# A two-layer decoder trunk: the last norm's output turned token by token on TensorE, fourteen products of ones ahead of the first chunk, and three steps of a key compression set one chunk further apart

## The chip, the cores and the metric

The kernel runs on one core of one Trainium2 chip. The metric is the device time of one execution in microseconds (us). A profiled execution also has a span, from its first to its last recorded event; times inside a profile count from the start of that span. TensorE is written PE (PEld for its weight loads), VectorE DVE, ScalarE ACT, GpSimd POOL and SyncE SP.

## The reference, cut to what matters

One sequence of 256 tokens with 2048 features runs through two layers: a mixer A (dilated attention), then a mixer B (compressed, selected and sliding-window attention over shared keys and values), each followed by an MLP and a gated per-layer embedding. The last thing computed is an RMSNorm over the 2048 features of each token.

```python
def reference(x, p, ...):
    h = x
    for i in range(DEPTH):
        hn = rmsnorm(h, attn_norm_g[i])
        ...                                   # mixer A (i = 0) or shared keys/values and mixer B (i = 1)
        hn = rmsnorm(h, mlp_norm_g[i])
        h = h + jnp.square(jax.nn.relu(hn @ mlp_w1[i])) @ mlp_w2[i]
        gate = jax.nn.sigmoid(rmsnorm(h, ple_norm_g[i]) @ ple_w_gate[i])
        h = h + (p[i] @ ple_w_proj[i]) * gate
    return rmsnorm(h, final_norm_g)
```

For mixer B, keys and values of 15 overlapping blocks of 32 tokens are compressed by a small MLP: a block's positions are flattened (`z`), multiplied by `w1`, passed through gelu and multiplied by `w2`; the keys are then rotated by position.

## The kernel before, in words

**Layout.** Activations lie features first: sixteen tiles `x[k]` of 128 features x 256 tokens in f32, held in eight pair tiles `xp[j]` of 512 columns. Weights come from HBM in chunks of 128 x 1024 f32 (512 KB), some 870 of them, through one loop (`Program.run`).

**Precision.** An f32 weight chunk `raw` becomes two parts: ACT casts the high part (`whi`, L196), DVE subtracts to get the low part (`wlo`, L202). Activations are split likewise (`xa`, L289 and L293). A product is high x (high and low) plus low x high (`mm_tile`, L318 and L319; `token_major`, L401 to L403).

**Order of the work.** `Program.run` walks over a list of steps written out by hand. At each chunk it issues loads up to `DMA_AHEAD` = 7 chunks ahead (with four raw buffers, so a load waits for the low part made from that buffer's earlier tenant), casts and subtracts up to `SPLIT_AHEAD` = 3 chunks ahead (fewer in the first chunks), advances the generators that finish earlier chunks by one `yield`, and then issues the chunk's products. A generator that yields `"tensor"` is resumed only after that chunk's products, so a `yield` more means one chunk more between a producer and TensorE's use of it. Every engine runs its own instructions in the order in which they were issued.

**The start.** `start0` (L565) issues the loads of the first two halves of `xp[0]`; `load` (L181) issues each raw chunk and, behind it, the next pair tile of `x`, all on SP's queue. `pieces` (L189) cuts chunk 0 into two halves, for its load, its cast and its subtraction; all others go whole. The first eight chunks are a value projection of layer A in `token_major` form: 12 products of 512 columns a chunk.

**The compression.** In `compress` (chunk by chunk, alternating with the chunks of a value projection through `both`), the key's eight chunks come first, then the value's. `gelu` (L864) finishes each: copy out of PSUM, a product with `pair` that adds the two halves (L870), gelu on 64 x 256, two transposes (L886), then `comp_k` (L899): the second product (L902), the rotation on DVE, a transpose (L916), and the split into the key tiles that the scores of mixer B read. The generators of the key's chain run while the value's chunks are being multiplied.

**The end.** The last quarter of the gate projection runs feature tile by feature tile (`single`); its last tile, `one_half=True`, accumulates all in 256 columns. `last_gate` (L492) then works out one long chain: the gate for tile 15 (L497 to L501), its square (L220), the sum over features by products with a vector of ones, which gives one value per token in two columns (`column`, L234), the root on ACT (L241), a reciprocal and one Newton step on DVE (L247 to L250, the factor `col`, one value per token on 128 partitions x 2 columns). Since the output is features first, the factor must lie along the columns: DVE builds a diagonal matrix from it (L253), and a product of ones with that diagonal (`spread`, L257) spreads it over all partitions. DVE multiplies the tiles by it in nine pieces (L511), and SP and ACT issue the nine writes to `out` in turn (L512). The host then transposes `out`.

Of the kernel before, what the change touches and what calls it, by code (L numbers as in the profile page):

```python
# [10 lines left out]
F32 = mybir.dt.float32  # L11
# [4 lines left out]
P = 128  # L16
D = 2048
T = 256
KT = D // P
# [10 lines left out]
CH = 1024  # L30
ROPE_SWAP = [(j + 16) % 32 for j in range(32)]

DMA_AHEAD = 7
SPLIT_AHEAD = 3
RAW_BUFS, HI_BUFS, LO_BUFS = 4, 6, 5
# [96 lines left out]
def kernel(ctx: ExitStack, tc: tile.TileContext, a: dict, out: bass.AP):  # L132
    nc = tc.nc
# [5 lines left out]
    stat = ctx.enter_context(tc.tile_pool(name="stat", bufs=2))  # L139
# [25 lines left out]
    xp = [xpool.tile([P, 2 * T], F32, name=f"x{j}") for j in range(KT // 2)]  # L165
    x = [xp[k // 2][:, k % 2 * T:(k % 2 + 1) * T] for k in range(KT)]
    ones = const.tile([P, P], F32, name="ones")
# [8 lines left out]
    def load_x(j, half=None):  # L176
        c = slice(0, 2 * T) if half is None else slice(half * T, (half + 1) * T)
        nc.sync.dma_start(xp[j][:, c], a["xT"][:, j * 2 * T:(j + 1) * 2 * T][:, c])
# [9 lines left out]

    def pieces(n):  # L189

        return [slice(0, CH // 2), slice(CH // 2, CH)] if n == 0 else [slice(0, CH)]

    def copy(n, t):
        hi = wpool.tile([P, CH], F32R, tag="hi", name="whi", bufs=HI_BUFS)
# [11 lines left out]
    class Norm:  # L206
# [19 lines left out]
                (eng or nc.vector).tensor_add(self.acc, self.acc, s)  # L226
            self.done += 1

        def column(self, parts):

            ps = banks2()[:, 0, :] if parity[0] else bank()
            for j in range(2):
                for i, p in enumerate(parts):
                    nc.tensor.matmul(ps[:, j:j + 1], p[:, j * P:(j + 1) * P], ones[:, :1],  # L234
                                     start=i == 0, stop=i == len(parts) - 1)
            return ps
# [3 lines left out]
            nc.vector.tensor_scalar(self.v, ps[:, :2], 1.0 / D, EPS, op0=ALU.mult, op1=ALU.add)  # L240
            nc.scalar.activation(self.z, self.v, AF.Sqrt)  # L241

        def invert(self):

            v, z = self.v, self.z
            y, r = (stat.tile([P, 2], F32, tag=n, name=n) for n in ("sy", "col"))
            nc.vector.reciprocal(y, z)  # L247
            nc.vector.tensor_mul(z, y, y)
            nc.vector.scalar_tensor_tensor(z, z, -0.5, v, op0=ALU.mult, op1=ALU.mult)
            nc.vector.scalar_tensor_tensor(r, z, 1.5, y, op0=ALU.add, op1=ALU.mult)  # L250
            self.diag = stat.tile([P, T], F32, tag="diag", name="diag", bufs=1)
            for j in range(2):
                nc.vector.tensor_scalar_mul(self.diag[:, j * P:(j + 1) * P], ident, r[:, j:j + 1])  # L253
            self.col = r

        def spread(self, ps):
            nc.tensor.matmul(ps[:, 128:128 + T], ones, self.diag, start=True, stop=True)  # L257
# [231 lines left out]
    def ple(layer, pg, xg, norm, nxt, norm2, last):  # L489
        pj = [None] * KT  # L490

        def last_gate(ps):  # L492

            k = KT - 1
            prog.until(lambda: norm2.done == k)
            t = tmp.tile([P, T], F32, tag="et", name="et", bufs=7)
            nc.vector.tensor_mul(t, ps[:, :T], norm.rb)  # L497
            nc.scalar.activation(t, t, AF.Sigmoid)
            nc.scalar.activation(warm, ones[:, :1], AF.Sqrt)
            nc.vector.tensor_mul(t, t, pj[k])  # L500
            nc.vector.tensor_add(x[k], x[k], t)  # L501
            s = norm2.square(k, nc.vector)
            col = norm2.column([norm2.acc, s])
            norm2.root(col)
            nc.scalar.activation(x[k], x[k], AF.Identity, scale=gains[:, G_FIN, k:k + 1])
            norm2.invert()
            r = norm2.spread(col)
            for i, (k0, n) in enumerate([(0, 1), (1, 1)] + [(2 * j, 2) for j in range(1, KT // 2)]):
                y = xp[k0 // 2][:, k0 % 2 * T:(k0 % 2 + n) * T]
                y3 = y.rearrange("p (n t) -> p n t", t=T)  # L510
                nc.vector.tensor_mul(y3, y3, r[:, None, :].to_broadcast([P, n, T]))  # L511
                (nc.sync, nc.scalar)[i % 2].dma_start(out[:, k0 * T:(k0 + n) * T], y)  # L512
            return
            yield

        def gate_done(k, ps):
            t = sum_halves(ps)
            for _ in range(k % 4 // 2):
                yield
            while norm.r is None:  # L520
                yield
            nc.vector.tensor_mul(t, t, norm.rb)
            yield
            nc.scalar.activation(t, t, AF.Sigmoid)
            yield
            nc.vector.tensor_mul(t, t, pj[k])
            nc.vector.tensor_add(x[k], x[k], t)
            yield
            if last or k < 12:
                s = norm2.square(k)  # L530
                if last:
                    nc.scalar.activation(x[k], x[k], AF.Identity, scale=gains[:, G_FIN, k:k + 1])
                yield
                norm2.add(s)
            else:
                yield from renorm(k, G_KV, nxt, norm2)

        for q in range(4):
            def proj_done(f, ps, q=q):
                s = tmp.tile([P, T], F32, tag="es", name="es", bufs=4)  # L540
                nc.scalar.copy(s, ps[:, :T])
                t = cur["h"].tile([P, T], F32, tag="pj", name="pj", bufs=8)
                nc.vector.tensor_add(t, ps[:, T:], s)
                pj[4 * q + f] = t
                return
                yield
            quad(lambda c, q=q: a["w_proj"][layer * 4 + q], 2, pg, proj_done)
            hooks = {4: [norm.factor]} if q == 0 else {}
            if q == 3 and not last:
                for c in range(6):  # L550
                    hooks[c] = [lambda k=k: split_x(k, G_KV, nxt) for k in (2 * c, 2 * c + 1)]
            if q == 3 and last:
                for f in range(4):
                    single(lambda c, f=f: a["w_gl"][2 * f + c], xg,
                           (lambda ps, k=12 + f: gate_done(k, ps)) if f < 3 else last_gate,
                           ring=lambda: banks2()[:, 0, :], one_half=f == 3)
            else:
                quad(lambda c, q=q: a["w_gate"][layer * 32 + q * 8 + c], KT, xg,
                     lambda f, ps, q=q: gate_done(4 * q + f, ps), hooks)
# [5 lines left out]
    def start0():  # L565
        load_x(0, 0)
        load_x(0, 1)
        open_pool("A")
        pa = cur["A"]
        cur["mA0"] = pa.tile([P, NGA * P], F32, name="mA0")  # L570
        cur["mA1"] = pa.tile([P, NGA * T], F32, name="mA1")
# [292 lines left out]
    def gelu(n, ps):  # L864
        s = tmp.tile([P, T], F32, tag="et", name="et", bufs=7)
        nc.scalar.copy(s, ps)
        yield
        yield "tensor"
        y = bank()[:64, :256]
        nc.tensor.matmul(y, pair, s, start=True, stop=True)  # L870
        yield
        t = tmp.tile([64, T], F32, tag="et", name="et", bufs=7)
        u = tmp.tile([64, T], F32, tag="et", name="et", bufs=7)
        nc.scalar.activation(t, y, AF.Square)
        yield
        nc.vector.tensor_scalar(t, t, 0.044715, 1.0, op0=ALU.mult, op1=ALU.add)
        nc.vector.tensor_mul(t, y, t)
        yield
        nc.scalar.activation(t, t, AF.Tanh, scale=math.sqrt(2.0 / math.pi))
        yield  # L880
        nc.vector.scalar_tensor_tensor(u, t, 1.0, y, op0=ALU.add, op1=ALU.mult)
        yield
        yield "tensor"
        ps = bank()
        for k in range(2):
            nc.tensor.transpose(ps[:, k * 64:(k + 1) * 64], u[:, k * P:(k + 1) * P], ident[:64, :64])  # L886
        yield
        if n == "k":
            uT = cur["B"].tile([P, P], F32, name="uT", tag="uT", bufs=1)
            nc.scalar.copy(uT, ps[:, :P])  # L890
        else:
            uT = cur["B"].tile([P, 8, 3, 16], F32, name="uT3")
            nc.scalar.copy(uT, ps[:, :P].rearrange("p (b n) -> p b n", n=16)[:, :, None, :]
                           .to_broadcast([P, 8, 3, 16]))
        yield
        yield "tensor"
        yield from (comp_k(uT) if n == "k" else comp_v(uT))

    def comp_k(uT):  # L899
# [10 lines left out]
        nc.vector.tensor_mul(w[:, 16:], kc[:, :16], zt["rcS"][:, 16:])  # L910
        nc.vector.tensor_mul(kc[:, :32], kc[:, :32], zt["rcC"])
        nc.vector.tensor_add(kc[:, :32], kc[:, :32], w)
        yield
        yield "tensor"
        ps = bank()
# [329 lines left out]
```

## Time and profile before

| What | us |
|---|---|
| Median of three timed runs | 2523.98 (2523.86 to 2524.05) |
| The profiled execution's own time | 2523.56 |
| Its span | 2521.8 |
| PE busy | 2502.3 |
| DVE busy | 1719.2 |
| ACT busy | 1339.7 |

Busy time is summed over the instructions of an engine. "Idle before" an instruction is shown with what released it, for instance `<-PE at L234`: the DVE instruction waited for a product at line 234. A row such as `L234 PE MATMUL at<-ones,acc 128*128 128x1 f32 x4` is four records of a product that writes tile `at`, reads moving operand `ones` and stationary operand `acc`; an f32 product is recorded as two. Products are pipelined, so the distance between their starts says more than their lengths. The rows of a windows view give for each stretch its length, the busy time and the count of each engine, then PEclk (the granted TensorE clock as a share of full speed), the DMA share and GB/s.

### The profile page before, as it was taken

Reading aid. Unit: us, or ns where it says so; the run is one execution under the profiler, and the core shown is the slowest. Engines: PE = TensorE matmul, PEld = TensorE weight load, DVE = VectorE, ACT = ScalarE, POOL = GpSimd, SP = SyncE. Lnnn points to the kernel's source line nnn. Section 1 sums busy time; section 2 is a strip of 40 time slices with the busy share of each in tenths; the row PEclk is TensorE's granted clock in tenths of the full one; section 3 lists DMA queues with packets and bytes.
Section 4 is the critical chain, followed back from the end, with each engine's and each line's share of the span. In section 5 each row is a group of like instructions: output and inputs, shape, how many; then the busy total and the mean of one; then the engine's idle time right before and its main releaser. Section 6 shows DMA issues by size and latency. Waiting matters only on the chain.

```text
span 2521.8 us, 37917 instructions
## 1 busy us (share of the span) xinstructions
PE 2502.3 (99%) x14399; PEld 2198.0 (87%) x14399; DVE 1719.2 (68%) x3005; ACT 1339.7 (53%) x2146; POOL 10.4 (0%) x24
## 2 busy tenths in 40 slices
PE   9999999999999999999999999999999999999997
PEld 7888888888888888888888889888888888888887
DVE  6766677866566665567787989776656556556777
ACT  6444444554354453455564788655435445445555
POOL 0000000000000000000000000000000000000000
PEclk9999999999999999999999999999999999999999
DMA  7555555566666666566566754456666666666663
GB/s 265 175 177 180 172 164 177 176 187 191 189 189 191 192 187 191 191 190 187 186 198 191 243 159 125 142 189 186 191 191 189 189 190 191 190 189 191 191 185 118
DMA packets 129831, 466.23 MB, mean 185 GB/s; under 512 B 14576, under 2 KB 15600, under 8 KB 129648
## 3 DMA queue, kind: packets, MB, share of 16 engines
q1 hardware_dynamic: 128400, 461.76, 58.7%
q8 instruction: 113, 1.85, 0.3%
q0 software_dynamic: 528, 1.07, 0.2%
q10 hardware_dynamic: 720, 0.98, 0.1%
q14 instruction: 70, 0.57, 0.1%
HBM read 461.65 MB, written 2.10 MB: 184 GB/s over the span
## 4 chain that ended last, share of the span: by engine, by line
PE 99%; DVE 1%; DMA 0%; issue 0%; ACT 0%; SPq 0%; DVEq 0%
PE mm L318 31%; PE at L318 26%; PE mm L319 16%; PE at L319 13%; PE mm L403 1%; PE mm L401 1%; PE mm L402 1%; PE at L401 1%; PE at L402 1%; PE at L403 1%; PE at L1092 0%; PE at L635 0%; PE mm L1116 0%; PE mm L855 0%; PE mm L856 0%; PE mm L688 0%
## 5 line engine op out<-in xcount | busy, mean ns | idle before, releaser
L202 DVE TENSOR_TENSOR wlo<-raw,whi 128x1024 fp32r<-128x1024 f32 (+1 forms) x874 | 1065.1, 1220 | 623.6 <-PE at L319 242.1
L196 ACT CAST whi<-raw 128x1024 fp32r<-128x1024 f32 (+1 forms) x874 | 920.3, 1054 | 914.6 <-PE at L318 407.7
L318 PE MATMUL mm<-xa,whi 128*128 128x512 f32 x2176 | 766.4, 396 | 0.0
L319 PE MATMUL mm<-xa,wlo 128*128 128x256 f32 x2176 | 608.8, 280 | 0.0
L318 PE MATMUL at<-xa,whi 128*128 128x512 f32 x1648 | 573.6, 392 | 0.0
L318 PEld LDWEIGHTS mm<-xa,whi 128*128 128x128 f32 x2176 | 407.9, 187 | 92.6 <-issue 0.4
L319 PE MATMUL at<-xa,wlo 128*128 128x256 f32 x1648 | 461.1, 280 | 0.0
L319 PEld LDWEIGHTS mm<-xa,wlo 128*128 128x128 f32 x2176 | 410.8, 189 | 0.4
L318 PEld LDWEIGHTS at<-xa,whi 128*128 128x128 f32 x1648 | 308.3, 187 | 68.0
L318 PE MATMUL mm<-h,whi 128*128 128x512 f32 x1024 | 355.7, 391 | 0.0
L318 PE MATMUL at<-h,whi 128*128 128x512 f32 x1024 | 355.7, 391 | 0.0
L319 PEld LDWEIGHTS at<-xa,wlo 128*128 128x128 f32 x1648 | 311.3, 189 | 0.1
L319 PE MATMUL mm<-h,wlo 128*128 128x256 f32 x1024 | 286.7, 280 | 0.0
L319 PE MATMUL at<-h,wlo 128*128 128x256 f32 x1024 | 286.7, 280 | 0.0
L318 PEld LDWEIGHTS at<-h,whi 128*128 128x128 f32 x1024 | 191.5, 187 | 42.0
L318 PEld LDWEIGHTS mm<-h,whi 128*128 128x128 f32 x1024 | 191.5, 187 | 42.0
L319 PEld LDWEIGHTS mm<-h,wlo 128*128 128x128 f32 x1024 | 193.5, 189 | 0.0
L319 PEld LDWEIGHTS at<-h,wlo 128*128 128x128 f32 x1024 | 193.5, 189 | 0.0
L325 DVE TENSOR_TENSOR et<-mm,es 128x256 f32<-128x256 f32 x137 | 55.7, 421 | 83.0 <-ACT es L323 80.9
L323 ACT COPY es<-mm 128x256 f32<-128x256 f32 x137 | 48.3, 371 | 67.5 <-PE mm L319 64.6
L325 DVE TENSOR_TENSOR et<-at,es 128x256 f32<-128x256 f32 x103 | 43.4, 422 | 36.7 <-ACT es L323 31.2
L323 ACT COPY es<-at 128x256 f32<-128x256 f32 x103 | 37.7, 370 | 51.8 <-DVE et L325 40.3
(292 smaller groups left out, 2372.3 us busy)
## 6 DMA issues: line engine op xcount, KB each, us to landing
raw<-in_w SPq DMA_DIRECT2D x512, 512.0 KB, 3.5
raw<-in_w_qk SPq DMA_DIRECT2D x96, 512.0 KB, 3.6
raw<-in_w_gate SPq DMA_DIRECT2D x56, 512.0 KB, 3.6
raw<-in_w_kv SPq DMA_DIRECT2D x48, 512.0 KB, 4.2
raw<-in_w_v SPq DMA_DIRECT2D x47, 512.0 KB, 3.6
raw<-in_w_q SPq DMA_DIRECT2D x32, 512.0 KB, 4.3
raw<-in_w_oB SPq DMA_DIRECT2D x32, 512.0 KB, 3.6
raw<-in_w_oA SPq DMA_DIRECT2D x16, 512.0 KB, 3.6
```

Source lines behind the costliest of these rows:

```text
L196: nc.scalar.copy(hi[:, c], t[:, c])
L202: nc.vector.tensor_sub(lo[:, c], t[:, c], f32(hi)[:, c])
L318: nc.tensor.matmul(ps, hi[:, col:col + P], rhs, start=first, stop=False)
L319: nc.tensor.matmul(ps[:, :T], lo[:, col:col + P], rhs[:, :T], start=False, stop=last)
L323: nc.scalar.copy(s, ps[:, :T])
L325: nc.vector.tensor_add(t, ps[:, T:], s)
L401: nc.tensor.matmul(st[j], xh, wh, start=k == 0, stop=False)
L402: nc.tensor.matmul(st[j], xl, wh, start=False, stop=False)
L403: nc.tensor.matmul(st[j], xh, wl, start=False, stop=k == KT - 1)
```

## The change

Four edits.

1. *Start.* `start0` issues 14 products of the 128 x 128 tile of ones with itself into a PSUM bank that nothing reads. `pieces` now cuts chunk 1 into halves as well.
2. *Compression.* The key's chain gets one more `yield` before its product with `pair`, one before its two transposes, and one before the last transpose. One chunk's products more lie between each producer and the step on TensorE; as compression and value chunks alternate, that is half of such a pair.
3. *The last norm.* The output is now tokens first: 128 partitions x (2 halves of tokens x 2048 features). TensorE transposes the sixteen scaled tiles of `x` (32 transposes of 128 x 128) into eight PSUM banks: twenty of them ahead of the column's products, the other twelve behind. Four of the banks are the ring `mm`, four are the two double banks that the last gate tile's ring now hands out (`last_ring`); the column's products go to one of these. The factor is then already in the place where it is needed, one value per partition, so the diagonal and its product are gone (`invert(False)`, no `spread`).
4. *The output.* Ten pieces (four of 128 KB, six of 256 KB) are scaled out of PSUM by DVE and ACT in turn, and all ten writes are issued by SP. The shape of `out` changes; the host's transpose with it.

On PE, what moves besides: the key's four small steps come one chunk later in order (its second product too, being behind the others). DVE and ACT make the key's gelu and rotation operations correspondingly later between the same casts and subtractions.

```diff
+WARM_UP = 14
...
-        return [slice(0, CH // 2), slice(CH // 2, CH)] if n == 0 else [slice(0, CH)]
+        return [slice(0, CH // 2), slice(CH // 2, CH)] if n < 2 else [slice(0, CH)]
...
-        def column(self, parts):
+        def column(self, parts, ps=None):
-            ps = banks2()[:, 0, :] if parity[0] else bank()
+            if ps is None:
+                ps = banks2()[:, 0, :] if parity[0] else bank()
...
-        def invert(self):
+        def invert(self, diag=True):
...
-            self.diag = stat.tile([P, T], F32, tag="diag", name="diag", bufs=1)
-            for j in range(2):
-                nc.vector.tensor_scalar_mul(self.diag[:, j * P:(j + 1) * P], ident, r[:, j:j + 1])
             self.col = r
+            if diag:
+                self.diag = stat.tile([P, T], F32, tag="diag", name="diag", bufs=1)
+                for j in range(2):
+                    nc.vector.tensor_scalar_mul(self.diag[:, j * P:(j + 1) * P], ident, r[:, j:j + 1])
...
             prog.until(lambda: norm2.done == k)
+            y, z = (last_banks[n] for n in ("y", "z"))
             t = tmp.tile([P, T], F32, tag="et", name="et", bufs=7)
             nc.vector.tensor_mul(t, ps[:, :T], norm.rb)
+            turned = {}
+
+            def turn(j, k0, to, kn=4):
+                for i in range(k0, k0 + kn):
+                    nc.tensor.transpose(to[:, i % 4 * P:(i % 4 + 1) * P], x[i][:, j * P:(j + 1) * P], ident)
+                turned[j, k0 // 4] = to
+
+            for q in range(2):
+                for j in range(2):
+                    turn(j, 4 * q, bank())
+            turn(0, 8, y[:, 0, :])
             nc.scalar.activation(t, t, AF.Sigmoid)
...
-            col = norm2.column([norm2.acc, s])
+            col = z[:, 1, :]
+            norm2.column([norm2.acc, s], col)
             norm2.root(col)
             nc.scalar.activation(x[k], x[k], AF.Identity, scale=gains[:, G_FIN, k:k + 1])
-            norm2.invert()
-            r = norm2.spread(col)
-            for i, (k0, n) in enumerate([(0, 1), (1, 1)] + [(2 * j, 2) for j in range(1, KT // 2)]):
-                y = xp[k0 // 2][:, k0 % 2 * T:(k0 % 2 + n) * T]
-                y3 = y.rearrange("p (n t) -> p n t", t=T)
-                nc.vector.tensor_mul(y3, y3, r[:, None, :].to_broadcast([P, n, T]))
-                (nc.sync, nc.scalar)[i % 2].dma_start(out[:, k0 * T:(k0 + n) * T], y)
+            turn(1, 8, y[:, 1, :])
+            turn(0, 12, z[:, 0, :])
+            norm2.invert(False)
+            turn(1, 12, z[:, 1, :])
+            r = norm2.col
+            for i, (q, j, c0, c1) in enumerate([(0, 0, 0, 256), (0, 1, 0, 256), (0, 0, 256, 512), (0, 1, 256, 512)] +
+                                               [(q, j, 0, 512) for q in range(1, 4) for j in range(2)]):
+                ps = turned[j, q][:, c0:c1]
+                o = xp[2 * q + j][:, c0:c1]
+                if i % 2:
+                    nc.scalar.mul(o, ps, r[:, j:j + 1])
+                else:
+                    nc.vector.tensor_scalar_mul(o, ps, r[:, j:j + 1])
+                c = j * D + q * 512
+                nc.sync.dma_start(out[:, c + c0:c + c1], o)
...
+        last_banks = {}
+
+        def last_ring():
+            last_banks["z"] = banks2()
+            last_banks["y"] = banks2()
+            return last_banks["z"][:, 0, :]
...
-                           ring=lambda: banks2()[:, 0, :], one_half=f == 3)
+                           ring=last_ring if f == 3 else lambda: banks2()[:, 0, :], one_half=f == 3)
...
         load_x(0, 1)
+        ps = bank()
+        for _ in range(WARM_UP):
+            nc.tensor.matmul(ps[:, :P], ones, ones, start=True, stop=True)
...
         nc.scalar.copy(s, ps)
         yield
+        if n == "k":
+            yield
         yield "tensor"
         y = bank()[:64, :256]
...
         nc.vector.scalar_tensor_tensor(u, t, 1.0, y, op0=ALU.add, op1=ALU.mult)
         yield
+        if n == "k":
+            yield
         yield "tensor"
...
         nc.vector.tensor_add(kc[:, :32], kc[:, :32], w)
         yield
+        yield
         yield "tensor"
```

More of the change, by code (lines that the diff above doesn't have):

```diff
@@ L1238 @@
             for n, v in laid.items()}
-    out = nc.dram_tensor("out_0", (P, KT * T), F32, kind="ExternalOutput").ap()
+    out = nc.dram_tensor("out_0", (P, T // P * D), F32, kind="ExternalOutput").ap()
     with _tile.TileContext(nc) as tc:
@@ L1243 @@
     y = r.results[0]["out_0"]
-    return np.ascontiguousarray(y.reshape(P, KT, T).transpose(2, 1, 0).reshape(1, T, D))
+    return np.ascontiguousarray(y.reshape(P, T // P, D).transpose(1, 0, 2).reshape(1, T, D))
```

## The prediction

> **What bounds the kernel now.** I read the page first, then TensorE's own waits, then the two ends in order of time.
>
> ```profile
> PE 2502.3 (99%) x14399; PEld 2198.0 (87%) x14399; DVE 1719.2 (68%) x3005; ACT 1339.7 (53%) x2146; POOL 10.4 (0%) x24
> ```
>
> ```profile
> PE at L401 <- ACT whi L196: 6.0, 1, 6.0
> PE at L234 <- DVE sq L220: 2.2, 1, 2.2
> PE at L257 <- DVE diag L253: 1.8, 1, 1.8
> ```
>
> TensorE is busy for 2502.3 of 2521.8 us. The waits view lists three gaps of more than 1 us: 6.0 before its first product, and 2.2 and 1.8 inside the last norm; after its last product the output is scaled and written. Between those ends there is nothing for a change off TensorE to win, unless it takes products away. So this change must be priced at the two ends, and its middle part by whether it makes TensorE wait.
>
> The start. The PE rows show when the products came to full speed:
>
> ```profile
> 10.02 0.63 PE L401 MATMUL at<-whi,xa 128*128 128x512 f32 x1
> 10.44 0.52 PE L402 MATMUL at<-whi,xa 128*128 128x512 f32 x1
> 10.80 0.39 PE L403 MATMUL at<-wlo,xa 128*128 128x512 f32 x1
> 11.03 0.40 PE L401 MATMUL at<-whi,xa 128*128 128x512 f32 x1
> ```
>
> Starts are 0.42 us apart up to 10.44 and 0.23 apart from 10.80 on: the clock doubled near 10.7 us, 4.7 us after the first product. Chunk 0 (12 products) ran at half rate nearly to its end; chunk 1 began at 11.03. The half rate cost some 11 x 0.2 = 2.2 us. Whether all of it can be had back depends on what the products would then wait for:
>
> ```profile
> 0.83 0.17 DVE L168 MEMSET ones<- 128x128 f32 x1 [0.83 <-PEq L1234]
> ...
> 5.99 0.69 DVE L202 TENSOR_TENSOR wlo<-raw,whi 128x512 fp32r<-128x512 f32 x1 [0.99 <-ACT whi L196]
> ...
> 12.00 1.22 DVE L202 TENSOR_TENSOR wlo<-raw,whi 128x1024 fp32r<-128x1024 f32 x1
> ...
> 13.94 1.22 DVE L202 TENSOR_TENSOR wlo<-raw,whi 128x1024 fp32r<-128x1024 f32 x1
> ```
>
> ```profile
> 8.97 1.04 ACT L196 CAST whi<-raw 128x1024 fp32r<-128x1024 f32 x1 [0.45 <-DMA raw<-in_w_v]
> ```
>
> ```profile
> raw<-in_w_v SPq DMA_DIRECT2D x1, 512.0 KB, 6.9
> ```
>
> The last row is the load of chunk 2, issued at 4.01 (SP rows below): it lands at 10.91, its cast follows at once, and its low part (the DVE row at 12.00) is ready at 13.22. Chunk 3's is ready at 15.16. These times are set by the loads, not by TensorE.
>
> **The change part by part.** *Fourteen products of ones.* They need only the memset that ends at 1.00. A product of two f32 128x128 tiles is two records:
>
> ```profile
> 95.09 0.39 PE L634 MATMUL mm<-qk 128*128 128x128 f32 x2
> 95.31 0.38 PE L635 MATMUL at<-qk 128*128 128x256 f32 x1
> ```
>
> 0.22 us at full rate, so 0.44 at half. Fourteen take 6.1 us at most, from about 1.05 to 7.1. If the clock rises 4.7 us after PE's first work, as above, it does so at 5.75; the products then end near 6.4. The first real product is free at 6.01, so it starts between 6.01 and 7.1, and runs at full rate.
>
> Follow the products at 0.23 from 6.4: chunk 0 ends at 6.4 + 12 x 0.23 = 9.2 (its first low part, ready at 6.68, is earlier than needed, and the second half's is one such operation behind). *Chunk 1 in two halves*: a half is 0.69 against 1.22 for the low part, so by that share about 0.6 against 1.04 for the cast. Even if its first half lands no earlier than the whole did (8.97), its high part is there at 9.6 and its low part at 10.3, which chunk 1's third product needs; ten more at 0.23 end chunk 1 at 12.6. Chunk 2's third product then waits for 13.22, and chunk 2 ends at 13.25 + 10 x 0.23 = 15.5. Before, it ended at 11.03 + 24 x 0.23 = 16.5. With a start at 7.1 instead of 6.4 the chain still stands at 13.25, since chunk 1 then ends by 12.7. Chunk 3's low part (15.16) is ahead of its need (15.9). **Start: -1.0 us.** Chunk 2's load hides the rest of the 2.2. The split adds one issue to SP's queue ahead of chunk 2's load:
>
> ```profile
> 3.06 0.43 SPq L184 DMA_DIRECT2D raw<-in_w_v  x1
> 3.53 0.43 SPq L178 DMA_DIRECT2D x<-in_xT  x1
> 4.01 0.47 SPq L184 DMA_DIRECT2D raw<-in_w_v  x1
> ```
>
> That is 0.47 later for everything behind it. A load that lands 6.9 us after its issue stands in a queue of bytes, so I take nothing for it. Bounds: -2.2 (nothing waits and all of the half rate comes back) and -0.5 (the 0.47 shows in full).
>
> *Key's compression.* Three steps of the key's chain move behind one more chunk. No instruction is added. Today's cost at the first of them:
>
> ```profile
> 1424.34 0.28 PE L856 MATMUL mm<-wlo,z 128*128 128x256 f32 x1
> 1424.55 0.65 PE L870 MATMUL mm<-et,pair 128*64 128x256 f32 x2
> ```
>
> The gap is 0.21 where such products follow each other at 0.12: at most 0.1 us is a wait. I take 0. What covers the moved vector and scalar work is that low parts are made two or more chunks ahead; without that cover one late low part would cost its 1.22 us. Bounds -0.3 (three such gaps) and +1.2. The keys themselves are read several chunks later, by the first scores.
>
> *The tail.* All times here are in the clock of before.
>
> ```profile
> 2508.37 0.43 DVE L220 TENSOR_TENSOR sq<-x 128x256 f32<-128x256 f32 x1
> ...
> 2509.98 0.16 DVE L240 TENSOR_SCALAR sv<-at 128x2 f32<-128x2 f32 x1 [1.19 <-PE at L234]
> ...
> 2511.20 0.48 DVE L253 TENSOR_SCALAR diag<-ident,col 128x128 f32<-128x128 f32 x2
> 2513.00 0.42 DVE L511 TENSOR_TENSOR x<-x,at 128x256 f32<-128x256 f32 x1 [1.31 <-PE at L257]
> ```
>
> Up to the square (ends 2508.80) nothing on the path changes. Twenty transposes now stand in TensorE's order ahead of the column's products:
>
> ```profile
> 2506.34 0.28 PE L234 MATMUL at<-ones,acc 128*128 128x1 f32 x2
> ```
>
> ```profile
> 108.15 0.27 PE L663 MATMUL at<-ident,p 128*128 128x128 f32 x1
> 108.26 0.27 PE L664 MATMUL at<-ident,p 128*128 128x128 f32 x1
> ```
>
> The first row is where TensorE came free. f32 transposes of this very form follow each other at 0.11, so twenty end at 2506.34 + 2.2 = 2508.54, 0.26 before the square: hidden. The column's first product then fills that gap; six records remain after the square. Before, they ran at the half rate to which the clock fell in the idle stretch:
>
> ```profile
> 2505.00:2510.00 5.00, 2.72 (x21) 2.55 (x19) 1.72 (x5) 1.90 (x3) 0.00 (x0) 0.93 0.00 0
> 2510.00:2515.00 5.00, 1.22 (x2) 0.50 (x2) 3.28 (x12) 0.60 (x2) 0.00 (x0) 0.50 0.14 47
> ```
>
> PEclk is 0.93, then 0.50. At full rate a column looks like this:
>
> ```profile
> 55.52 0.50 PE L234 MATMUL mm<-ones,acc 128*128 128x1 f32 x4
> 55.89 0.48 PE L318 MATMUL mm<-xa,whi 128*128 128x512 f32 x1
> ```
>
> Four records in 0.50 us, 0.09 apart; six take 0.68, so sv starts at 2508.85 + 0.71 = 2509.56 instead of 2509.98: **-0.4**. From sv to the first reader of the factor is 1.22 us on either side (2509.98 to 2511.20). The diagonal and its product, 2511.20 to 2513.00, go: **-1.8**. The first scaling starts at 2510.78 instead of 2513.00, 2.2 earlier. [...] No row of this kernel shows a column right behind transposes alone. [...]
>
> What is late next is the output. Ten pieces are scaled on two engines instead of nine on one, so scaling, which paced the issues before, takes about half its time. All ten issues are SP's now, where SP had five of nine, the last over at 2513.45 + 4.84 = 2518.29:
>
> ```profile
> 2513.45 4.84 SPq L512 DMA_DIRECT2D out<-x  x5
> ```
>
> ```profile
> 2519.50:2520.00 0.50, 0.00 (x0) 0.00 (x0) 0.00 (x0) 0.00 (x0) 0.00 (x0) 0.50 1.03 389
> 2520.00:2520.50 0.50, 0.00 (x0) 0.00 (x0) 0.00 (x0) 0.00 (x0) 0.00 (x0) 0.50 0.11 37
> ```
>
> The DMA engines are full at 389 GB/s and stop at about 2520.05, 6.6 us after the first issue; 2.1 MB alone need 5.4. So the writes pace the end. The first issue comes 0.45 after the first scaling starts (2513.00 to 2513.45), now at 2511.23. On SP alone the first four pieces (128 KB, 0.34 us at 389 GB/s) come at an issue's 0.47: up to 4 x 0.13 = 0.5 us is lost, part of it already in the 6.6, where the first pieces are small too. I take 0.1, bounds 0 and 0.5. **Tail: -2.2 + 0.1 = -2.1**, bounds -2.4 and -1.3 (column at half rate, 0.5 lost).
>
> *Sum*: -1.0 + 0 - 2.1 = -3.1 us. The profiled execution took 2523.56 us (span 2521.8 and 1.8 around it) and would take 2520.5. The median shown is 2523.98, 0.4 higher; set against that median the forecast is 2523.98 - 3.1 = **2520.9 us**. All bounds at one side give -0.6 and -4.9; as its own range I take 2519.7 to 2522.3, since the terms are independent.
>
> **The rivals.**
> 1. *The transposes leave the clock low.* Price: the 0.4 of the column, 2521.3. For it: the clock did fall in that idle stretch before. Against: it fell only near 2509.3 (0.93 over 5 us is 0.7 us at half), and by then the column would be nearly done. 0.10. [...]
> 2. *The products of ones do not raise the clock.* Then they only push the first real product to 7.1; half rate lasts to 10.7, 8.4 products; chunk 0 ends at 10.7 + 3.6 x 0.23 = 11.5 instead of 11.03: start +0.5, total -1.6, 2522.4. For it: no row shows such products raising it. Against: any products did it before. 0.08.
> 3. *SP's issues pace the output.* From a pitch of about 0.52 on, the tenth issue is late. At 0.8 (an issue plus a wait for each engine in turn) it starts at 2511.23 + 7.2 = 2518.4, about where SP's last one ended before; the tail gives 0, total -1.0, 2523.0. Against: 0.43 to 0.47 at the start. 0.06.
> 4. *Slower: transposes one at a time.* If each holds TensorE for a weight load (2198.0 us for 14399 loads on the page, 0.15 each) and its whole 0.27, 0.42 in all, twenty end at 2514.7 and the column starts 5.9 late: -3.1 + 5.9 = +2.8, 2526.8. It costs from a pitch of 0.12 on and makes the kernel slower from 0.28 on. Against: 0.11 in the rows above. 0.04.
> 5. *The whole 2.2 of the half rate comes back*, because halves make loads land sooner: 2.2 + 2.1 = 4.3, 2519.7. Against: bytes pace chunk 2. 0.05.
>
> **How the numbers follow.** The forecast has 0.61, and 0.06 is left for what no case holds. The range must hold eight in ten: the forecast and cases 1, 2 and 5 (0.84) lie within 2519.5 to 2522.8, so that is the range. A time can be told from no change when it differs by 0.2%, 5.0 us. No case named reaches that; of the 0.06 I put 0.03 on faster and 0.03 on slower, and 0.94 stay within.
>
> **What would show it.** In the changed profile: PE records of ones from about 1.05; real products 0.23 apart by 8 us and chunk 2 done about 1 us earlier; DVE's low part of chunk 2 still near 13.2. PE rows around the key's pair product without a gap over 0.3. Twenty transposes 0.11 apart that end before the square does; six records of the column in about 0.7; first scaling 1.2 us after sv; SP issues at most 0.47 apart; DMA full until the end. The prediction is wrong if the column starts later than 0.1 us after the square, if the first chunks still run 0.43 apart after 8 us, or if DMA falls idle between pieces.

## The result, and the profile after

The changed kernel takes 2519.77 us (median of 20 runs, 2519.42 to 2520.12); the kernel before, beside it, 2524.20 us (20 runs, 2523.31 to 2525.69). The ratio is 0.9982 with a 95% interval of 0.9976 to 0.9989: 4.4 us or 0.18% faster, just inside the 0.2% that the prediction called the limit of what can be told. The interval lies wholly below 1; what the single parts of it are worth is read from the traces. The profiled execution took 2519.91 us (span 2518.1).

The page of the changed kernel, engines; then TensorE's own waits (who waited, for whom; us in total, times, longest):

```profile
PE 2507.3 (100%) x14457; PEld 2204.1 (88%) x14457; DVE 1716.8 (68%) x3000; ACT 1342.8 (53%) x2152; POOL 10.4 (0%) x24
```

```profile
PE mm L605 <- DVE ones L169: 1.1, 1, 1.1
PE at L406 <- DVE wlo L203: 0.4, 1, 0.4
PE at L1086 <- DVE ko L434: 0.3, 1, 0.3
```

The gaps of 6.0, 2.2 and 1.8 us are gone. In the first place stand the products of ones, whose result nothing reads; the clock came to full at 7.16 here, near 10.7 in before. The start, PE rows in order of time:

```profile
1.05 0.58 PE L605 MATMUL mm<-ones 128*128 128x128 f32 x1 [1.05 <-DVE ones L169]
...
7.05 0.53 PE L404 MATMUL at<-whi,xa 128*128 128x512 f32 x1
7.42 0.40 PE L405 MATMUL at<-whi,xa 128*128 128x512 f32 x1
7.65 0.40 PE L406 MATMUL at<-wlo,xa 128*128 128x512 f32 x1
...
13.66 0.50 PE L406 MATMUL at<-wlo,xa 128*128 128x512 f32 x1 [0.37 <-DVE wlo L203]
```

All 28 records of ones ran at half rate (0.21 us a record, from 1.05 to 7.05; 0.11 in the prediction's row at full rate) and held TensorE until 7.05; from the second real product on, products are 0.23 apart. The third product of chunk 2 waits 0.37 for its low part, which is ready at 13.61 here ("near 13.2" was expected). The end, PE rows, then DVE rows, then SP's issues:

```profile
2504.45 1.91 PE L510 MATMUL mm<-ident,x 128*128 128x128 f32 x16
2506.19 0.60 PE L510 MATMUL at<-ident,x 128*128 128x128 f32 x4
2506.63 0.28 PE L236 MATMUL at<-ones,acc 128*128 128x1 f32 x2
2506.95 0.38 PE L236 MATMUL at<-ones,sq 128*128 128x1 f32 x2
...
2507.64 1.79 PE L510 MATMUL at<-ident,x 128*128 128x128 f32 x12
```

```profile
2506.47 0.42 DVE L221 TENSOR_TENSOR sq<-x 128x256 f32<-128x256 f32 x1
2507.82 0.16 DVE L242 TENSOR_SCALAR sv<-at 128x2 f32<-128x2 f32 x1 [0.92 <-PE at L236]
2509.04 1.54 DVE L538 TENSOR_SCALAR x<-mm,col 128x256 f32<-128x256 f32 x3
```

```profile
2509.55 5.06 SPq L540 DMA_DIRECT2D out<-x  x10
```

The twenty transposes are 0.11 apart and over before the square is (2506.89). From the column's first record behind the square to sv it is 0.87. The first scaling comes 1.22 after sv, and no diagonal lies between. The windows of the end (length, busy times and counts of PE, PEld, DVE, ACT and POOL, then PEclk, DMA share, GB/s):

```profile
2510.50:2511.00 0.50, 0.00 (x0) 0.00 (x0) 0.50 (x2) 0.01 (x1) 0.00 (x0) 1.00 0.81 268
...
2512.50:2513.00 0.50, 0.00 (x0) 0.00 (x0) 0.00 (x0) 0.17 (x1) 0.00 (x0) 0.55 1.04 389
...
2516.00:2516.50 0.50, 0.00 (x0) 0.00 (x0) 0.00 (x0) 0.00 (x0) 0.00 (x0) 0.50 0.97 365
2516.50:2517.00 0.50, 0.00 (x0) 0.00 (x0) 0.00 (x0) 0.00 (x0) 0.00 (x0) 0.50 0.04 12
```

DMA is not full while the four 128 KB pieces go out (268 GB/s), and is afterwards (389). SP's ten issues, the last at 2514.03, begin 0.50 apart on average, where the prediction's sign was at most 0.47. The clock fell near 2512.5 (PEclk 0.55 in the window from there, 0.50 behind), 3.1 us after the end of TensorE's last record (2509.43).

**Three stretches.** To see where the time went, each profile is cut at two instructions: the first transpose of layer A's heads (108.15 in before, quoted in the prediction) and DVE's first operation of the last gate (the first rows below are after's, the last is before's).

```profile
107.76 0.27 PE L701 MATMUL at<-ident,p 128*128 128x128 f32 x1
```

```profile
2504.65 0.42 DVE L505 TENSOR_TENSOR et<-at,sr 128x256 f32<-128x256 f32 x1 [2.18 <-PE at L378]
```

```profile
2506.54 0.42 DVE L497 TENSOR_TENSOR et<-at,sr 128x256 f32<-128x256 f32 x1 [2.18 <-PE at L375]
```

| Kernel (profiled execution) | start | middle | tail | span | median less before's beside it |
|---|---|---|---|---|---|
| before | 108.15 | 2398.39 | 15.26 | 2521.8 | |
| rot_only | 108.53 | 2398.29 | 15.58 | 2522.4 | +0.15 |
| compress_only | 108.95 | 2398.29 | 14.66 | 2521.9 | -0.06 |
| pad_pe | 108.38 | 2398.30 | 15.62 | 2522.3 | -0.28 |
| pad_act | 107.91 | 2398.42 | 14.77 | 2521.1 | +0.28 |
| pad_sp | 108.51 | 2398.46 | 16.64 | 2523.6 | +0.89 |
| start_only | 107.32 | 2399.20 | 15.57 | 2522.1 | -1.51 |
| tail_only | 109.00 | 2396.93 | 13.47 | 2519.4 | -2.98 |
| after | 107.76 | 2396.89 | 13.45 | 2518.1 | -4.43 |
| after_pad_dve | 107.90 | 2396.89 | 13.41 | 2518.2 | -4.50 |
| turn_behind | 107.71 | 2396.91 | 13.58 | 2518.2 | -2.83 |
| after_whole_chunk1 | 108.33 | 2396.93 | 13.55 | 2518.8 | -4.09 |
| after_two_issuers | 107.08 | 2396.89 | 13.04 | 2517.0 | -4.91 |
| after_best | 107.24 | 2396.92 | 13.04 | 2517.2 | -5.64 |

The start of one and the same program scatters by about 1 us from run to run, so one profile of each kernel can't price it: before's and after's own differ by 0.39 there. Seven profiles without the start's edit have a mean of 108.49 (107.91 to 109.00), five with the whole of it (start_only, after, after_two_issuers, after_pad_dve, turn_behind) one of 107.55 (107.08 to 107.90): **-0.94**, by this scatter good to some 0.2 (standard error). The middle is sharp: 2398.3 to 2398.5 with the old last norm (start_only apart), 2396.9 with the new one: **-1.45**. The tail, worked out from the span as printed to 0.1, has a mean of 15.24 with the old norm (six profiles, pad_sp left out for its added writes), and 13.45 in after: **-1.8**. The sum, -4.2, agrees with the medians' -4.43; the middle was in no sum of the prediction.

### The profile page after: what moved, and what is told of

It reads as the page before. It is cut to its first block, busy times and chain, and to the rows that moved or that the text cites. A ratio compares the mean times of both kernels' runs of the same rounds, so it can differ in the third digit from the quotient of the medians.

```text
span 2518.1 us, 38042 instructions
## 1 busy us (share of the span) xinstructions
PE 2507.3 (100%) x14457; PEld 2204.1 (88%) x14457; DVE 1716.8 (68%) x3000; ACT 1342.8 (53%) x2152; POOL 10.4 (0%) x24
## 4 chain that ended last, share of the span: by engine, by line
PE 99%; DVE 0%; DMA 0%; SPq 0%; ACT 0%; issue 0%; DVEq 0%
PE mm L321 31%; PE at L321 26%; PE mm L322 16%; PE at L322 14%; PE mm L404 1%; PE mm L406 1%; PE mm L405 1%; PE at L406 1%; PE at L404 1%; PE at L405 1%; PE at L1135 0%; PE at L673 0%; PE mm L1159 0%; PE mm L893 0%; PE mm L894 0%; DMA raw<-in_w_v 0%
```

## The experiments

Eleven runs per kernel; the interval of a ratio is about 0.0009 to either side, 2.2 us, so a difference of medians under that is a hint, and the verdicts rest on the traces.

### One part at a time

**start_only**: before with the first edit alone.

```diff
-        return [slice(0, CH // 2), slice(CH // 2, CH)] if n == 0 else [slice(0, CH)]
+        return [slice(0, CH // 2), slice(CH // 2, CH)] if n < 2 else [slice(0, CH)]
...
+        ps = bank()
+        for _ in range(WARM_UP):
+            nc.tensor.matmul(ps[:, :P], ones, ones, start=True, stop=True)
```

> Only the start's edit: 14 products of ones and chunk 1 in halves. By the trace of after, the first chunks give -0.4 us by the end of chunk 2 (forecast on record: -1.0). Theory A (phase): the 1.36 us that after gained between 171 and 418 us, where pairs of products at the QKV line run at 346.5 instead of 353.3 ns, comes from where TensorE's stream stands when it resumes after a head's transposes, moved by the start. Theory B (ring): it comes from the one PSUM bank that the products of ones take, which turns the ring mm by one place. Theory C (chance): the pitch differs from run to run and belongs to no edit. A and B: about -1.8 us in all, with the same units at 346.5 as in after. C: -0.4 in the mean, and the units at 346.5 are others than in after.

Measured: 2522.72 us, ratio 0.9994 (0.9985 to 1.0003). The middle shows none of after's gain, so A and B both fail here. It shows a loss instead, +0.8 against the other kernels with the old norm. PE and DVE rows of start_only, then of before, at the last transpose of the key's chain:

```profile
1444.05 0.28 PE L860 MATMUL mm<-wlo,z 128*128 128x256 f32 x1
1444.96 0.24 PE L920 MATMUL mm<-ident,kc 64*128 64x64 f32 x1 [0.63 <-DVE kc L916]
```

```profile
1444.63 0.18 DVE L916 TENSOR_TENSOR kc<-kc,kcr 64x32 f32<-64x32 f32 x1
```

```profile
1444.88 0.28 PE L856 MATMUL mm<-wlo,z 128*128 128x256 f32 x1
1445.09 0.27 PE L916 MATMUL mm<-ident,kc 64*128 64x64 f32 x1
```

```profile
1444.63 0.18 DVE L912 TENSOR_TENSOR kc<-kc,kcr 64x32 f32<-64x32 f32 x1
```

DVE finishes `kc` at 1444.81 in both. TensorE, 0.83 earlier, now has to wait for it: in this profile most of the start's gain is given back 1440 us later. But the profiled run is one of three (2523.50 to 2523.89) that lie some 1.1 us above the other eight (2522.44 to 2522.95), and those eight are 1.3 to 1.8 below before's median, more than the start's whole gain as measured: they show no such loss, and no trace of them is kept. Nor does an earlier TensorE always have to wait here: in tail_only the same product starts at 1444.36, 0.52 earlier than in before, `kc` is finished at 1444.32, 0.49 earlier, and there is no wait.

**compress_only**: before with the three `yield`s alone.

```diff
+        if n == "k":
+            yield
         yield "tensor"
         y = bank()[:64, :256]
```

> Only the three yields of the key's compression. Forecast on record: 0 (bounds -0.3 and +1.2). By the trace of after: -0.14 between 1425 and 1455 us, which no measurement of the whole can tell from 0. Theory A and B: all pitches before 1424 us as in before. Theory C: they can differ, by up to 1.4 us either way.

Measured: 2524.17 us, ratio 0.9999 (0.9990 to 1.0008), middle 2398.29: at most -0.1. Alone the edit is worth nothing that can be seen. In the seven profiles that have it (compress_only, after and the five made from after), the transpose of `kc` starts 0.32 after the record ahead of it, without a wait, and `kc` is finished more than 3 us ahead of it, against 0.28 in before.

**tail_only**: before with the last norm's edit alone (the diff's third and fourth part).

```diff
+            for q in range(2):
+                for j in range(2):
+                    turn(j, 4 * q, bank())
...
+            norm2.invert(False)
...
+                nc.sync.dma_start(out[:, c + c0:c + c1], o)
```

> Only the last norm's edit: transposes into PSUM, the factor used per token, ten writes by SP. Forecast on record: -2.1 us. By the trace of after: -1.8 (column -0.26, diagonal and its product -1.8, later start and output together the rest with +0.45 lost to the writes). Theory A and B: nothing in the middle, so -1.8 in all and pitches as in before. Theory C: pitches can differ, by up to 1.4 us either way. If instead the transposes only hid behind the clock that the start's shift had moved, the column would be late here: the clock would fall near 2509.3 as in before, and the column's -0.26 would go, -1.5.

Measured: 2521.25 us, ratio 0.9989 (0.9981 to 0.9998). The tail is 13.47, as in after. The middle is after's too, though every instruction of the edit stands behind it: up to the last norm this kernel and before have the same instructions, in the same order and at the same on-chip addresses, on all five engines. PE rows of one stretch of QKV products, the same 22 pairs (high, then low part) in before and in tail_only:

```profile
169.42 0.40 PE L318 MATMUL mm<-xa,whi 128*128 128x512 f32 x1
...
177.19 0.40 PE L318 MATMUL mm<-xa,whi 128*128 128x512 f32 x1
```

```profile
170.26 0.40 PE L321 MATMUL mm<-xa,whi 128*128 128x512 f32 x1
...
177.88 0.40 PE L321 MATMUL mm<-xa,whi 128*128 128x512 f32 x1
```

7.77 us against 7.62, or 353 ns a pair against 346. Of the stretches behind the seven heads' transposes, those behind heads 1, 3, 4 and 6 run at the shorter pitch with the new norm and at the longer with the old; behind head 0 both have the shorter, behind 2 and 5 both the longer. (The expectations name heads 0, 3 and 6, which was misread.)

**rot_only**: before with one bank taken in the start, chunk 1 whole.

```diff
+WARM_UP = 1
...
+        ps = bank()
+        for _ in range(WARM_UP):
+            nc.tensor.matmul(ps[:, :P], ones, ones, start=True, stop=True)
```

> One bank of the ring mm is taken in the start and one product of ones writes it; it is over by 1.6 us, long before the first chunk, so the first chunks stand as before (0.0 at the end of chunk 2). Theory B (ring): -1.36 us, with the units after the transposes of heads 0, 3 and 6 at 346.5 ns a pair, as in after. Theory A (phase): 0 +/-0.2, pitches as in before. Theory C (chance): pitches that follow neither.

Measured: 2524.38 us, ratio 1.0000 (0.9991 to 1.0009), all pitches as in before. B fails. C fails as well, as far as one profile of each kernel can tell: of fourteen profiles, each of the seven with the old norm has the one pattern of pitches and each of the seven with the new norm the other, to within 1 ns a pair.

### What of the last norm reaches back 2000 us?

Each engine's count of instructions was tried by itself: **pad_sp** (before, SP's five writes cut into twelve), **pad_pe** (before, sixteen products of ones behind the last product), **pad_act** (before, eight one-column copies at ACT's end) and **after_pad_dve** (after, eight at DVE's end).

```diff
-                (nc.sync, nc.scalar)[i % 2].dma_start(out[:, k0 * T:(k0 + n) * T], y)
+                if i % 2:
+                    nc.scalar.dma_start(out[:, k0 * T:(k0 + n) * T], y)
+                else:
+                    h = n * T // (4 if i == 8 else 2)
+                    for c in range(0, n * T, h):
+                        nc.sync.dma_start(out[:, k0 * T + c:k0 * T + c + h], y[:, c:c + h])
```

```diff
+            pad = bank()
+            for _ in range(16):
+                nc.tensor.matmul(pad[:, :P], ones, ones, start=True, stop=True)
```

```diff
+            for _ in range(8):
+                nc.scalar.copy(warm, ones[:, :1])
```

```diff
+            for _ in range(8):
+                nc.vector.tensor_copy(warm, ones[:, :1])
```

> Before, with SP's five writes of the output cut into twelve; nothing else. The runs so far left theories A (phase), B (ring) and C (chance) without support: the pitches of the QKV pairs followed the last norm's edit, whose instructions come 2000 us later. Up to there the kernels' instructions and addresses are the same. Theory D: it is the number of instructions or transfers that SP has in all (before 5 writes on SP; after 10). D: the middle as in after, -1.36 between 171 and 418 us; the tail's seven more issues on SP cost up to 7 x 0.47 of which the wait for the scalings hides most, so +0.5 to +1.5 there. Theory E (TensorE's count of instructions): middle as in before, 0.

> Before, with 16 products of ones (32 records, as many as the 30 that the last norm's edit adds to TensorE) issued behind its last product, beside the output. Theory E: -1.36 in the middle, -1.36 in all, since the added products lie beside the writes. Theory D: pitches as in before, 0 in all.

> Before, with eight one-column copies on ACT behind everything else. Theories D (SP's count) and E (TensorE's count) fell: twelve writes on SP and 32 records more on TensorE left the pitches as in before, and five writes on SP left those of after. What the last norm's edit changes beside these is ACT's count (+3 to +10 instructions) and DVE's (-6). Theory F (ACT's count): -1.36 us between 171 and 418 us, as in after. Theory G (DVE's count): as in before, 0.

> After, with eight one-column copies on DVE behind its last scaling, so that DVE has as many instructions as in before again. They lie beside the writes and cost nothing. Theory G: the middle returns to before's pitches, +1.36 against after. Theory F, or a cause outside the counts: the middle as in after, 0.

Measured: 2525.30, 2524.13, 2524.64 and 2519.86 us (ratios 1.0002, 0.9999, 1.0001, 0.9983). No middle changed: the first three keep before's 2398.3 to 2398.5, the last after's 2396.89. D, E, F and G all fail, and the cause stays open. What wasn't tried is several counts at once, the length of all programs together, where program and tensors lie in memory, and what one execution leaves behind in TensorE for the next. Pad_sp also priced seven more issues on SP: from the first scaling to the span's end 9.8 us instead of 8.8.

### The output

**after_two_issuers**: after with the ten writes issued in turn.

```diff
-                nc.sync.dma_start(out[:, c + c0:c + c1], o)
+                (nc.sync, nc.scalar)[i % 2].dma_start(out[:, c + c0:c + c1], o)
```

> After, with the ten writes issued by SP and ACT in turn, as before's nine were. The forecast on record took 0.1 us for ten writes on SP alone (bound 0.5); the trace of after has DMA at 268 GB/s while the 128 KB pieces come, so about 0.45 lost. If SP's issues are what is late: -0.4 against after, with DMA near 380 GB/s from the first pieces on. If not: 0. Beside that theory D: SP's count falls back to five writes, so the middle returns to before's pitches, +1.36, net +0.9 against after. Theory E: middle as in after, net -0.4.

Measured: 2519.50 us, ratio 0.9981 (0.9972 to 0.9990). Windows of the end, first scaling at 2508.35:

```profile
2510.00:2510.50 0.50, 0.00 (x0) 0.00 (x0) 0.50 (x2) 0.26 (x1) 0.00 (x0) 1.00 1.02 338
2510.50:2511.00 0.50, 0.00 (x0) 0.00 (x0) 0.50 (x2) 0.43 (x1) 0.00 (x0) 1.00 1.01 334
...
2515.00:2515.50 0.50, 0.00 (x0) 0.00 (x0) 0.00 (x0) 0.00 (x0) 0.00 (x0) 0.50 0.80 303
2515.50:2516.00 0.50, 0.00 (x0) 0.00 (x0) 0.00 (x0) 0.00 (x0) 0.00 (x0) 0.50 0.00 0
```

DMA is busy throughout from 2510.0, at 334 GB/s and more where after has 268, and the tail is 13.04 instead of 13.45: -0.41. One issuer was what held the small pieces.

### The start and the place of the transposes

**after_whole_chunk1**: after with `pieces` as in before.

```diff
-        return [slice(0, CH // 2), slice(CH // 2, CH)] if n < 2 else [slice(0, CH)]
+        return [slice(0, CH // 2), slice(CH // 2, CH)] if n == 0 else [slice(0, CH)]
```

> After, with chunk 1 whole again: tests the split of the start's edit. Chunk 1's low part is then ready near 11.25 (landing near 9.0, cast 1.04, low part 1.23) where its third product could start near 10.3; ten more products end it at 13.6, chunk 2 ends at 16.3 if its own low part is no later: +0.2 against after. If SP's added issue (0.47) was what held the start, chunk 2's load lands 0.47 earlier: -0.2 to -0.4 against after. The landing of chunk 2's load has so far differed by 0.8 us from run to run (10.90 to 11.73), so only the rows within the run, and the median of many, can tell. Middle as in after by both D and E.

Measured: 2520.32 us, ratio 0.9984 (0.9976 to 0.9993). TensorE waits for chunk 1's low part; PE row, and DVE row of that low part:

```profile
11.58 0.50 PE L406 MATMUL at<-wlo,xa 128*128 128x512 f32 x1 [0.53 <-DVE wlo L203]
```

```profile
10.30 1.22 DVE L203 TENSOR_TENSOR wlo<-raw,whi 128x1024 fp32r<-128x1024 f32 x1 [1.41 <-ACT whi L197]
```

It waits for chunk 1's high part as well, 0.3 by the waits view. The start is 108.33 against a mean of 107.55 with the split: in this one profile, without the split, only 0.16 of the 0.94 is left. The two waits (0.8 together) account for the difference; the medians, each against before's beside it (-4.09 against -4.43), put it at 0.3. That the split matters is seen, how much is not settled. The issue saved on SP gained nothing that can be seen: chunk 2's cast began at 11.17, within the range of the runs that have it.

**turn_behind**: after with all 32 transposes behind the column.

```diff
-            for q in range(2):
-                for j in range(2):
-                    turn(j, 4 * q, bank())
-            turn(0, 8, y[:, 0, :])
             nc.scalar.activation(t, t, AF.Sigmoid)
...
+            for q in range(2):
+                for j in range(2):
+                    turn(j, 4 * q, bank())
+            turn(0, 8, y[:, 0, :])
             turn(1, 8, y[:, 1, :])
```

> After, with all 32 transposes behind the column's products, so that TensorE idles ahead of the column as in before. The forecast had twenty of them hidden ahead of the square, and the clock held up by them. If they are hidden either way (32 x 0.11 = 3.5 us from the column's end, while the scalings of ten pieces take 3.6 us from 1.2 us after sv): 0 to +0.3 against after. If transposes do not count as work for the clock (rival 1), it falls within the column or the transposes, which then run at 0.21: the last ends some 3 us later and the last pieces wait, +1 to +3. [...]

Measured: 2521.53 us, ratio 0.9986 (0.9977 to 0.9995), but in two groups: four of eleven runs at 2519.5 to 2520.0, as after, the others at 2521.5 to 2522.9. The profiled run is of the lower group. Its PE rows and windows:

```profile
2507.61 3.10 PE L510 MATMUL mm<-ident,x 128*128 128x128 f32 x16
2510.50 2.47 PE L510 MATMUL at<-ident,x 128*128 128x128 f32 x16
```

```profile
2504.80:2508.22 3.42, 1.68 (x14) 1.59 (x15) 1.68 (x6) 2.14 (x5) 0.00 (x0) 1.00 0.00 0
2508.22:2511.63 3.41, 3.41 (x19) 3.41 (x18) 2.27 (x7) 1.89 (x4) 0.00 (x0) 0.50 0.29 96
2511.63:2512.70 1.07, 1.07 (x11) 1.07 (x10) 0.56 (x1) 0.00 (x0) 0.00 (x0) 1.00 0.84 285
```

The clock was full up to 2508.22 (PEclk 1.00, TensorE busy for 1.68 of the 3.42 us), at half from there to 2511.63 (0.50) and full again behind it (1.00). In the 3.41 us at half TensorE did nothing but transposes, so the clock rose behind transposes alone here. What the upper group waits for has no trace here, so what it is worth to have twenty of them ahead of the column is seen in the medians only (-2.83 against after's -4.43, within the noise of a ratio).

**after_best**: after with two issuers, and `pieces` in halves for `n < 3`.

```diff
-        return [slice(0, CH // 2), slice(CH // 2, CH)] if n < 2 else [slice(0, CH)]
+        return [slice(0, CH // 2), slice(CH // 2, CH)] if n < 3 else [slice(0, CH)]
...
-                nc.sync.dma_start(out[:, c + c0:c + c1], o)
+                (nc.sync, nc.scalar)[i % 2].dma_start(out[:, c + c0:c + c1], o)
```

> After, with the writes issued by SP and ACT in turn (which in the run so far moved DMA's first 2 us to full rate, the median by about -0.3), and with chunk 2 in halves as well. In after, TensorE waits 0.37 us for chunk 2's low part; halves make the first of it ready about 1 us after its half lands. Expected -0.3 in the start if chunk 3's low part (ready at 15.54 in after) is not later for it, 0 if SP's further issue (0.47) makes it so; with the issuers -0.6 to -0.3 against after, about 2519.2.

Measured: 2518.72 us (eleven runs, 2518.36 to 2520.83), ratio 0.9978 (0.9969 to 0.9987); after_pad_dve, which is after but for eight idle copies, took 2519.86 in the same comparison. TensorE's waits don't have the 0.4 for chunk 2's low part:

```profile
PE at L404 <- ACT whi L197: 0.6, 1, 0.6
PE at L1086 <- DVE ko L434: 0.3, 1, 0.3
```

It has the lowest median of all kernels here, some 1.1 us below after's, of which the issuers' 0.4 is seen in the tail (13.04). What the halves of chunk 2 bring isn't shown: after_two_issuers, with chunk 2 whole, doesn't have the 0.4 in its waits either, and its start is 107.08 against 107.24 here. The 0.6 is the other side of the start: in this run the clock rose at 4.4 us, the products of ones were over sooner, and TensorE waited for its first chunk.

## Why the prediction held, and where it didn't

**The start (-1.0, measured -0.94, good to some 0.2)** came out as worked out: chunk 3's first product starts at 15.89 on average in the five profiles with the whole edit and at 16.83 in the seven without, so all of it is there by the end of chunk 2, and in four of the five chunk 2's third product waits for its low part (0.08 to 0.53). One link was wrong, which cost nothing. The clock did not rise 4.7 us after TensorE's first work here: in after it rose at 7.16, 6.1 us after. The 4.7 was one run's: the first rise lies between 9.6 and 12.0 in the seven profiles without the fourteen products, and between 4.4 and 7.2 in the seven with them. What sets its time within these is not shown. The prediction had allowed for a start at 7.1. Its reason for not counting SP's added issue held too: chunk 2's cast began at 11.22 on average without it (10.60 to 11.73), at 11.12 with it (10.65 to 11.48).

**"Nothing for a change off TensorE to win" in the middle** is the step that failed: -1.45 us, of which -1.35 lies in the pairs between 167 and 418 us. Nothing that the prediction shows of before's profile told it: the work is the same, and no engine waits. It is larger than the start's term, and its cause is not settled.

**Compression (0)**: right for the edit alone (-0.06). Whether it is worth something beside the start's edit is open. It was priced in the timeline of before, where `kc` is ready 0.28 ahead of its transpose; in the profile of start_only, with TensorE 0.83 earlier, that slack is gone and 0.63 is paid; in the seven profiles with the edit nothing waits there. But the medians of the three parts (-1.51, -0.06, -2.98) add up to -4.55, which agrees with after's -4.43: in the medians there is no loss for the edit to prevent. The bounds (-0.3 to +1.2) left out that the price can hang on another edit of the same change.

**The tail (-2.1, measured -1.8)**, by its terms. The diagonal and its product: 3.02 us from sv to the first scaling in before, 1.22 in after, -1.8 as forecast. The column: from the square's start to sv 1.62 in before, 1.35 in after, -0.27 instead of -0.4; over the seven profiles with the old norm the mean is 1.74 (1.34 to 1.96; the column's pairs of records behind the square stand 0.23 to 0.24 apart in pad_act and 0.43 to 0.45 in start_only, whose PEclk is 0.52 there), which gives -0.39. The forecast compared with before's own 1.62, and took 0.71 from the column's first record to sv, which measured 0.87. The output: from first scaling to the end of the span 8.8 in before, 9.1 in after. The +0.1 was too small by some 0.2, and after_two_issuers showed that it was the issues on one queue, the effect whose bound of 0.5 the prediction had worked out. DMA not full between the small pieces (a share of 0.81) was also one of its signs of being wrong, and it is where this term was.

**The rivals.** 1 (transposes leave the clock low) fell: the column took 1.34 or 1.35 from the square's start in all seven profiles with the new norm, the clock stayed full in after until 2512.5, and turn_behind's rose at 2511.63, after 3.41 us of transposes alone. 2 (ones don't raise it) fell: with the fourteen products the clock was up by 7.2 us in all seven profiles, without them nowhere before 9.6. 3 (SP's issues pace the output) was there, at 0.50 an issue, for some 0.4 us and not 2. 4 (transposes at 0.42) fell at 0.11. 5 (all of the 2.2) fell at 0.94.

So the 2519.77 came 1.1 below the forecast of 2520.9 because a gain that no step had (-1.45) outweighed a tail that brought 0.3 less than forecast. That it still lies in the range of 2519.5 to 2522.8 is luck in part: the range was built from cases at the two ends, and none of them is what moved the time.

## What to carry to other kernels

Price an edit that only adds distance between a producer and its reader in the timeline that the other edits make, not in that of before: there the slack may be gone, as in the one profile of start_only. Where a start depends on loads and on when the clock rises (4.4 to 7.2 us in the seven profiles with the fourteen products), one profile of each kernel is not enough; take several and compare means, or find a mark inside the run that both share. And cut a small difference into stretches by shared instructions before telling its story: here a third of it lay where no instruction had changed.

## What the runs showed of the hardware

- Programs that are the same, instruction for instruction, up to 2500 us ran products at two pitches (346 or 353 ns a pair) in the same places, the same in every profile of a kernel family, whatever the start's timing. By itself, none of SP's, TensorE's, ACT's or DVE's instruction counts changed it (pad_sp, pad_pe, pad_act, after_pad_dve).
- Before's time scatters more (2523.31 to 2525.69) than after's (2519.42 to 2520.12). In the profiles, the column of the old norm, which stands behind 2.2 us of TensorE's idle time, took 1.34 to 1.96 us from the square's start to sv, against 1.34 or 1.35 in all seven with the new one; the old one's pairs of records behind the square ran 0.23 to 0.24 apart in pad_act and 0.43 to 0.45 in start_only, at a PEclk of 0.52. That is 0.6 us, part of the 2.4 by which before's times differ.
- Under f32 transposes of 128 x 128 the clock stayed full in after (PEclk 1.00 from 2500 to 2510), and it rose from half to full at 2511.63 in turn_behind, after 3.41 us of transposes alone.
